# A modulation vector by products on VectorE instead of column sums on TensorE, and eleven matmuls of ones at the start

## The chip, the cores and the metric

The kernel runs on one core of a Trainium2 chip. The metric is the device time of one execution in microseconds (us), shown as the median of several runs.

## The reference, cut to what matters

Three blocks run one after the other on a sequence of 512 tokens with 1024 features: two layers of the first block (grouped-query band attention, short convolution, gated mix, SwiGLU feed-forward) and one layer of the second block, whose two halves are modulated by a vector that depends on an input `c` alone.

```
c_act = jax.nn.silu(c)
mod = c_act @ ada_w[l] + ada_b[l]          # c: 1024, ada_w: 1024 x 6144
sh_a, sc_a, gt_a, sh_m, sc_m, gt_m = jnp.split(mod, 6)
h = rmsnorm(x, norm_mix_g) * (1.0 + sc_a) + sh_a
...
x = x + gt_a * mixed
```

The change concerns `mod`, 6144 values, and nothing else of what is computed.

## The kernel before, in words

Activations lie with features on the partitions (tiles of 128 features x 512 tokens). Each weight matrix comes as units of 128x1024 fp32 words (512 KB). `Stream` loads a unit into one of three raw buffers (L255, queue of SyncE, SP), ScalarE makes its high part `wh` (L267), VectorE the remainder `wl` (L268), two units ahead of their use. A block of 128 output features (`mblock`, `mm_kb`) is 24 matmuls of 128x512: for each of eight tiles of the input the three products high x high (L523), low x high (L524) and high x low (L525).

The program is written in one order, and a scheduler then places each engine's instructions by a simulated timeline. So instructions stand on the engines in another order than in the source, and a small change of the source can move rows elsewhere. PSUM tiles outside attention take their buffers from two groups in the cycle of `CYC` (L331), one step for each tile that `ps` hands out.

`setup` (L338) issues the first loads: some columns, the first weight unit, four tiles of the input `x`, two more units, constants. It fills a 128x128 tile `ones` (L357). `ada_start` (L895) makes `ca`, silu of `c` as 8 columns of 128, by seven short VectorE operations and one Exp on ScalarE (`sigmoid_small`, L383).

The modulation is spread over `ffn1` (L706), the feed-forward part of each layer of the first block. It loops over 22 tiles of the hidden width, each with two blocks: the gate (L718 on VectorE times the norm, SiLU on ScalarE, L720 on GpSimd), and the up projection (L723 product, L516 the low part). In tiles 2 to 13 of each layer `ada_step` (L906) is called twice, 48 times in all. One step takes a tile `adaraw` of 128x1024 (128 rows of `ada_w`, 1024 of its columns), multiplies each partition by its value of `ca` and adds the result to `adaacc` (L918 for the first of eight, L920 for the other seven), then loads the next tile (L934). After eight steps the sum over the 128 partitions is still open: eight matmuls with `adaacc` as the stationary operand and one column of `ones` as the moving one (L927) give 8 columns of 128 sums, and VectorE adds the bias (L930). Six such groups, three in each layer, give `mod` as 128 x 48. The profile counts each fp32 matmul as two instructions.

Tiles of 128x1024 words, `adaraw` and `adaacc` among them, come from one pool of 39 buffers (`blk`).

Of the kernel before, what the change touches and what calls it, by code (L numbers as in the profile page):

```python
# [9 lines left out]
F32 = mybir.dt.float32  # L10
F32R = mybir.dt.float32r
AF = mybir.ActivationFunctionType
OP = mybir.AluOpType

P = 128
T = 512
D = 1024
NB = 8
# [5 lines left out]
NF = FF // P  # L24
# [4 lines left out]
U = 1024  # L29
# [3 lines left out]
def col_layout():  # L33
    off, lay = 0, {}

    def add(name, n):
        nonlocal off
        lay[name] = (off, n)
        off += n

    for l in range(DEPTH):
        for n in ("g_pre_mix", "g_post_mix", "g_pre_ffn", "g_post_ffn"):
            add(f"{n}{l}", NB)
        add(f"conv_w{l}", 3 * NB)
        add(f"sink{l}", NH)
    for n, c in (("c", NB), ("ada_b", 48), ("nmg", NB), ("nfg", NB), ("fcw", 3 * NF), ("fcb", NF), ("dgq", 1),
                 ("dgk", 1), ("lam", P), ("subg", 1), ("fgq", 1), ("fgk", 1), ("fbf", 4), ("ngq", 1), ("ngk", 3),
                 ("pe", 32)):
        add(n, c)
    return lay, off  # L50
# [9 lines left out]
def fm_cols(v):  # L60
    v = np.asarray(v)
    return v.reshape(-1, P).T
# [20 lines left out]
def pack(inp):  # L83
# [20 lines left out]
    o = np.cumsum([0, 256, 256, 256, 256, 256, 256, 4, 256, 256, 256, 256, 64, 64, 64, 64, 64, 64, 12])  # L104
# [7 lines left out]
    g = cat(dvs, dvw, bf, dg, dks, dkw)  # L112
    g = np.concatenate([g.reshape(NB, P, 272), np.zeros((1, P, 272), g.dtype)]).reshape(3, 3, P, 272)
    g = g.transpose(0, 2, 1, 3).reshape(3, P, 816)
# [7 lines left out]
    put(np.stack([fm_units(up[:, :FF]), fm_units(up[:, FF:])], axis=1).reshape(2 * NF, P, U))  # L122
    put(down_units(inp["ffn_w_down_2"][0]))
    lay, nc_ = col_layout()
    cols = np.zeros((P, nc_), np.float32)

    def setc(name, v):
        o, n = lay[name]
        cols[:, o:o + n] = v

    for l in range(DEPTH):
# [1 line left out]
            setc(f"{n}{l}", fm_cols(inp[n][l]))  # L133
        setc(f"conv_w{l}", fm_cols(inp["conv_w"][l]))
        setc(f"sink{l}", np.tile(inp["attn_sink"][l][None, :], (P, 1)))
    setc("c", fm_cols(inp["c_2"][0]))
    setc("ada_b", fm_cols(inp["ada_b_2"][0]))
    setc("nmg", fm_cols(inp["norm_mix_g_2"][0]))
    setc("nfg", fm_cols(inp["norm_ffn_g_2"][0]))
# [36 lines left out]
    for i in range(2):  # L176
# [4 lines left out]
    c, s = np.cos(ang).astype(np.float32).T, np.sin(ang).astype(np.float32).T  # L181
# [12 lines left out]
        "onehot": onehot,  # L194
        "tab": np.ascontiguousarray(tab, np.float32),
        "phi": phib.reshape(P, 32 * P),
        "ada": np.asarray(inp["ada_w_2"])[0].reshape(NB, P, 6, U).transpose(2, 0, 1, 3).reshape(48, P, U),
        "x": np.ascontiguousarray(np.asarray(inp["x"])[0].T.reshape(NB, P, T).transpose(1, 0, 2).reshape(P, NB * T)),
    }

# [79 lines left out]
class Kern:  # L280
# [31 lines left out]
    def small(self, name, shape, dt=F32, bufs=3):  # L312
        return self.smp.tile(shape, dt, name=self.n(name), tag=name, bufs=bufs)

    TAIL = 4
    NHF = 4
    NH3 = 4
# [20 lines left out]
    def setup(self):  # L338
        nc = self.nc
        self.cols = self.cpool.tile([P, self.ncol], F32, name="cols")  # L340
        nc.sync.dma_start(self.cols[:, :NB], self.a["cols"][:, :NB])
        xin = self.a["x"].rearrange("p (j a t) -> p j a t", j=4, a=2)
        self.xsrc = [[xin[:, j, :, t0:t1] for j in range(4)] for t0, t1 in HV]
        self.xpre = {}
        self.st.load_to(1)
        for j in range(4):
            self.xpre[0, j] = self.xload(0, j)
        self.st.load_to(3)
        self.cst = self.cpool.tile([P, 520], F32, name="cst")
        nc.sync.dma_start(self.cst, self.a["consts"])  # L350
        nc.sync.dma_start(self.cols[:, NB:], self.a["cols"][:, NB:])
        self.ident = self.cst[:, 0:P]
        self.band = self.cst[:, P:512]
        self.caus = self.cst[:, 384:512]
        self.valid = self.cst[:, 512:520]
        self.ones = self.cpool.tile([P, P], F32, name="ones")
        nc.vector.memset(self.ones, 1.0)  # L357
        self.mhalf = self.cpool.tile([P, 4], F32, name="mhalf")
        nc.vector.memset(self.mhalf, -0.5)
        self.R = self.cpool.tile([P, T], F32, name="R")  # L360
# [179 lines left out]
    def layer(self, l, tail, pend):  # L540
# [130 lines left out]
        acc = self.tmp("acc")  # L671
        m0 = NB - self.TAIL
        for m in range(m0):
# [219 lines left out]
        return F  # L893

    def ada_start(self):  # L895
        nc = self.nc
        self.ca = self.cpool.tile([P, NB], F32, name="ca")
        o, _ = self.lay["c"]
        c = self.cols[:, o:o + NB]
        self.sigmoid_small(self.ca, c, [P, NB])  # L900
        nc.vector.tensor_mul(self.ca, self.ca, c)
        self.mod = self.cpool.tile([P, 48], F32, name="mod")
        self.ada_i = 0
        self.ada_raw = None

    def ada_step(self):  # L906
        nc = self.nc
        i = self.ada_i
        if i >= 48:
            return  # L910
        self.ada_i += 1
        if i == 0:
            self.ada_load(0)
        t = self.ada_raw
        g, kb = divmod(i, NB)
        if kb == 0:
            self.ada_acc = self.blk("adaacc", [P, U], F32)
            nc.vector.tensor_scalar(self.ada_acc, t, self.ca[:, 0:1], None, op0=OP.mult)  # L918
        else:
            nc.vector.scalar_tensor_tensor(self.ada_acc, t, self.ca[:, kb:kb + 1], self.ada_acc, op0=OP.mult,  # L920
                                           op1=OP.add)
        if i + 1 < 48:
            self.ada_load(i + 1)
        if kb == NB - 1:
            ps = self.ps("ada")
            for m in range(NB):
                nc.tensor.matmul(ps[:, m:m + 1], self.ada_acc[:, m * P:(m + 1) * P], self.ones[:, 0:1], start=True,  # L927
                                 stop=True)
            o = self.lay["ada_b"][0] + g * NB
            nc.vector.tensor_add(self.mod[:, g * NB:(g + 1) * NB], ps[:, :NB], self.cols[:, o:o + NB])  # L930

    def ada_load(self, i):
        self.ada_raw = self.blk("adaraw", [P, U], F32)
# [258 lines left out]
    def block2(self, tail, pend):  # L1192
# [185 lines left out]

        m0 = NB - self.TAIL
        for m in range(m0):  # L1380
# [401 lines left out]
```

## Time and profile before

| | before |
|---|---|
| median of 3 runs | 2462.95 us (2461.41 to 2464.72) |
| the profiled execution | 2465.88 us |
| its span, first to last instruction | 2464.2 us |
| mean granted TensorE clock | 0.991 |
| busy: TensorE matmul | 2407.3 us (98%) |
| TensorE weight loads (beside the matmuls) | 2073.7 us (84%) |
| VectorE | 1324.1 us (54%) |
| ScalarE | 996.1 us (40%) |
| GpSimd | 399.2 us (16%) |

PE is the TensorE matmul, PEld its weight load, DVE VectorE, ACT ScalarE, POOL GpSimd and SPq the queue of SyncE that issues the DMAs. A row of the timeline gives start, duration, engine, line, operation, output and inputs, and a count where equal rows are merged; in square brackets stands the idle time before it and what ended it. Matmuls are pipelined: on a busy TensorE the step from one start to the next is the cost, not the duration.

### The profile page before, as it was taken

How to read it: one execution, taken by the hardware profiler on the slowest of the kernel's cores; microseconds unless marked ns; L12 is line 12 of the kernel's file. 1: busy time of each engine (PE TensorE's matmuls, PEld its weight loads, DVE VectorE, ACT ScalarE, POOL GpSimd, SP SyncE). 2: the span in 40 equal slices, each digit the busy share in tenths (PEclk: the TensorE clock that was granted, in tenths of full speed). 3: DMA queues.
4: the chain of work that ended last, by engine and by line, in shares of the span. 5: the costliest groups of instructions: out<-in, count | busy, mean ns of one | idle time of the engine just before them, and what ended most of it. 6: DMA issues, size and time to landing. Idle time of an engine off the chain costs nothing.

```text
span 2464.2 us, 32671 instructions
## 1 busy us (share of the span) xinstructions
PE 2407.3 (98%) x12680; PEld 2073.7 (84%) x12680; DVE 1324.1 (54%) x2324; ACT 996.1 (40%) x1808; POOL 399.2 (16%) x437
## 2 busy tenths in 40 slices
PE   8999999999999999999999999999898899999999
PEld 8888888888888898888888888888788878888888
DVE  6777544366533177775434655422667586644531
ACT  4555423442223245554224322322375575333420
POOL 3433001211110034230012111100021232000000
PEclk9999999999999999999999999999799999999999
DMA  4511523355423244223233553332221204233350
GB/s 159 149 61 64 165 94 103 103 196 200 149 85 121 80 144 126 69 83 99 94 98 129 181 195 137 99 107 74 91 88 53 83 22 146 78 103 103 105 171 24
DMA packets 90115, 272.77 MB, mean 111 GB/s; under 512 B 10175, under 2 KB 19007, under 8 KB 89960
## 3 DMA queue, kind: packets, MB, share of 16 engines
q1 hardware_dynamic: 89960, 270.68, 33.1%
q8 instruction: 100, 1.64, 0.3%
q14 instruction: 55, 0.45, 0.1%
HBM read 249.65 MB, written 15.22 MB: 107 GB/s over the span
## 4 chain that ended last, share of the span: by engine, by line
PE 90%; DVE 3%; ACT 3%; POOL 2%; issue 2%; DMA 0%; SPq 0%; POOLq 0%; ACTq 0%; DVEq 0%
PE ps L523 24%; PE ps L525 24%; PE ps L524 24%; PE hd L524 2%; PE hd L525 2%; PE hd L523 2%; PE o L840 2%; PE pt L815 1%; PE tm L1025 1%; PE tm L1026 1%; PE tm L1027 1%; POOL t L576 1%; POOL t L575 1%; ACT pp L378 1%; PE s L791 1%
## 5 line engine op out<-in xcount | busy, mean ns | idle before, releaser
L268 DVE TENSOR_TENSOR wl<-raw,wh 128x1024 fp32r<-128x1024 f32 x382 | 477.5, 1267 | 346.6 <-ACT wh L267 283.2
L267 ACT CAST wh<-raw 128x1024 fp32r<-128x1024 f32 x382 | 390.0, 1050 | 188.6 <-DMA raw<-in_w_dram 99.0
L525 PE MATMUL ps<-hh,wl 128*128 128x512 f32 x752 | 295.3, 393 | 0.9 <-DVE wl L268 0.8
L524 PE MATMUL ps<-hl,wh 128*128 128x512 f32 x752 | 294.9, 392 | 0.0
L523 PE MATMUL ps<-hh,wh 128*128 128x512 f32 x752 | 294.4, 392 | 0.0
L524 PE MATMUL ps<-hfl,wh 128*128 128x512 f32 x640 | 249.3, 390 | 0.0
L523 PE MATMUL ps<-hfh,wh 128*128 128x512 f32 x640 | 249.1, 390 | 0.0
L525 PE MATMUL ps<-hfh,wl 128*128 128x512 f32 x640 | 248.9, 389 | 0.0
L525 PEld LDWEIGHTS ps<-hh,wl 128*128 128x128 f32 x752 | 141.3, 188 | 29.1 <-DVE wl L268 2.1
L524 PEld LDWEIGHTS ps<-hl,wh 128*128 128x128 f32 x752 | 141.2, 188 | 27.2
L523 PEld LDWEIGHTS ps<-hh,wh 128*128 128x128 f32 x752 | 141.2, 188 | 27.1 <-ACT ot L844 0.2
L525 PE MATMUL ps<-hidh,wl 128*128 128x512 f32 (+1 forms) x396 | 145.1, 366 | 0.0
L523 PE MATMUL ps<-hidh,wh 128*128 128x512 f32 (+1 forms) x396 | 144.9, 366 | 0.0
L524 PE MATMUL ps<-hidl,wh 128*128 128x512 f32 (+1 forms) x396 | 144.7, 365 | 0.0
L378 ACT ACTIVATE pp<-pp,at_nm 128x256 f32<-128x256 f32 (+1 forms) x208 | 114.4, 553 | 68.2 <-DVE at_nm L797 60.0
L525 PEld LDWEIGHTS ps<-hfh,wl 128*128 128x128 f32 x640 | 120.1, 188 | 24.9
L524 PEld LDWEIGHTS ps<-hfl,wh 128*128 128x128 f32 x640 | 120.2, 188 | 24.7
L523 PEld LDWEIGHTS ps<-hfh,wh 128*128 128x128 f32 x640 | 120.0, 188 | 24.8
L720 POOL TENSOR_TENSOR gs<-gs,R 128x512 f32<-128x512 f32 x44 | 71.4, 1623 | 377.6 <-ACT gs L378 366.6
L524 PE MATMUL ps<-h3l,wh 128*128 128x512 f32 x320 | 124.5, 389 | 0.0
L525 PE MATMUL ps<-h3h,wl 128*128 128x512 f32 x320 | 124.5, 389 | 0.0
L523 PE MATMUL ps<-h3h,wh 128*128 128x512 f32 x320 | 124.3, 389 | 0.0
(461 smaller groups left out, 5200.3 us busy)
## 6 DMA issues: line engine op xcount, KB each, us to landing
raw<-in_w_dram SPq DMA_DIRECT2D x382, 512.0 KB, 3.7
adaraw<-in_ada_dram SPq DMA_DIRECT2D x48, 512.0 KB, 5.6
xd<-xh SPq DMA_DIRECT2D x24, 256.0 KB, 2.1
xh<-xd SPq DMA_DIRECT2D x24, 256.0 KB, 3.1
xh<-in_x_dram SPq DMA_DIRECT2D x16, 256.0 KB, 5.0
Q<-ql SPq DMA_DIRECT2D x32, 128.0 KB, 3.4
bias_d<-row_d SPq DMA_DIRECT2D x8, 320.0 KB, 7.5
KH<-kst SPq DMA_DIRECT2D x16, 128.0 KB, 3.9
```

Of the source, the lines that this page charges most:

```text
L267: nc.scalar.copy(hi, raw)
L268: nc.vector.tensor_sub(lo, raw, hi.bitcast(F32))
L378: i = nc.scalar.activation(out, in_, func, **kw)
L523: nc.tensor.matmul(ps[:, t], w[0][:, sl], h.hi[kb][:, t], start=first, stop=False)
L524: nc.tensor.matmul(ps[:, t], w[0][:, sl], h.lo[kb][:, t], start=False, stop=False)
L525: nc.tensor.matmul(ps[:, t], w[1][:, sl], h.hi[kb][:, t], start=False, stop=last)
L575: nc.gpsimd.tensor_mul(t2, t2, S)
L576: nc.gpsimd.tensor_add(t1, t1, t2)
L720: nc.gpsimd.tensor_mul(g, g, self.R)
L791: nc.tensor.matmul(ps[:, :n], q, KL[g][:, LO[i]:HI[i]], start=False, stop=True)
L815: nc.tensor.transpose(bank[:, c0:c0 + P], pslice(h, i)[:, c:c + P], self.ident)
L840: nc.tensor.matmul(ps[:, c0:c1], V[j][:, g * P:(g + 1) * P], t[b][:, a, c0:c1], start=(a == 0 and j == 0), stop=(a == 1 and j == 2))
```

## The change

The matrix `ada_w` is laid out transposed: tile i holds 128 of the 6144 output features on the partitions, and the 1024 inputs along the free axis. `c` comes as one row of 1024 words (`crow`) and is spread over all partitions by the DMA that loads it, once in each layer; SiLU is one operation of ScalarE on 128x1024. One step is then one VectorE instruction, `tensor_tensor_reduce`: product of the two tiles, summed along the free axis starting from the bias column, the sum going straight into a column of `mod`. The seven short operations of `ada_start`, the matmuls of L927 and the adds of L930 are gone. Apart from that, `setup` now issues eleven matmuls of `ones` by `ones` (128x128, fp32) into a PSUM tile `pw` that nobody reads.

```diff
+    WARM = 11
...
         nc.vector.memset(self.ones, 1.0)
+        ps = self.ps("pw")
+        for i in range(self.WARM):
+            nc.tensor.matmul(ps[:, :P], self.ones, self.ones, start=True, stop=True)
...
     def ada_start(self):
-        nc = self.nc
-        self.ca = self.cpool.tile([P, NB], F32, name="ca")
-        o, _ = self.lay["c"]
-        c = self.cols[:, o:o + NB]
-        self.sigmoid_small(self.ca, c, [P, NB])
-        nc.vector.tensor_mul(self.ca, self.ca, c)
         self.mod = self.cpool.tile([P, 48], F32, name="mod")
         self.ada_i = 0
-        self.ada_raw = None
...
         self.ada_i += 1
-        if i == 0:
-            self.ada_load(0)
+        if i % 24 == 0:
+            self.ca = self.blk("ca", [P, U], F32)
+            self.nc.sync.dma_start(self.ca, self.a["crow"].to_broadcast([P, U]))
+            self.act(self.ca, self.ca, AF.Silu)
+            self.ada_load(i)
         t = self.ada_raw
-        g, kb = divmod(i, NB)
-        if kb == 0:
-            self.ada_acc = self.blk("adaacc", [P, U], F32)
-            nc.vector.tensor_scalar(self.ada_acc, t, self.ca[:, 0:1], None, op0=OP.mult)
-        else:
-            nc.vector.scalar_tensor_tensor(self.ada_acc, t, self.ca[:, kb:kb + 1], self.ada_acc, op0=OP.mult,
-                                           op1=OP.add)
-        if i + 1 < 48:
+        if i % 24 < 23:
             self.ada_load(i + 1)
-        if kb == NB - 1:
-            ps = self.ps("ada")
-            for m in range(NB):
-                nc.tensor.matmul(ps[:, m:m + 1], self.ada_acc[:, m * P:(m + 1) * P], self.ones[:, 0:1], start=True,
-                                 stop=True)
-            o = self.lay["ada_b"][0] + g * NB
-            nc.vector.tensor_add(self.mod[:, g * NB:(g + 1) * NB], ps[:, :NB], self.cols[:, o:o + NB])
+        o = self.lay["ada_b"][0] + i
+        self.nc.vector.tensor_tensor_reduce(out=t, in0=t, in1=self.ca, scale=1.0, scalar=self.cols[:, o:o + 1],
+                                            op0=OP.mult, op1=OP.add, accum_out=self.mod[:, i:i + 1])
```

Three places show how the instructions stand now. Behind the added lines of `setup` the line numbers are four higher than before (L527 is L523 of before), behind `ada_start` lower.

TensorE at the start of the program, before (`hd` is the output of the first three blocks, `hh` and `hl` the parts of the normalised input):

```order
L1777 UNCONDITIONAL_BRANCH
L523 MATMUL hd_168<-hh_10_122,wh_8_116 128x256
L524 MATMUL hd_168<-hl_11_123,wh_8_116 128x256
L525 MATMUL hd_168<-hh_10_122,wl_9_117 128x256
L523 MATMUL hd_168<-hh_10_122,wh_8_116 128x256
```

The same place now:

```order
L1765 UNCONDITIONAL_BRANCH
L361 MATMUL pw_99<-ones 128x128 x11
L527 MATMUL hd_168<-hh_9_122,wh_7_116 128x256
L528 MATMUL hd_168<-hl_10_123,wh_7_116 128x256
L529 MATMUL hd_168<-hh_9_122,wl_8_117 128x256
```

The eleven matmuls stand ahead of all others on TensorE; behind them the order is as it was.

TensorE in `ffn1` of the first layer around the first of the six groups, before (`ps` is the PSUM tile of a block, `hfh` and `hfl` its input):

```order
L524 MATMUL ps_5131<-hfl_762_4474,wh_842_5039 128x512
L525 MATMUL ps_5131<-hfh_761_4473,wl_843_5040 128x512
L523 MATMUL ps_5131<-hfh_761_4473,wh_842_5039 128x512
L927 MATMUL ada_5115<-ones,adaacc_4878 128x1 x8
L524 MATMUL ps_5131<-hfl_762_4474,wh_842_5039 128x512
L525 MATMUL ps_5131<-hfh_761_4473,wl_843_5040 128x512
```

The same place now:

```order
L528 MATMUL ps_5124<-hfl_761_4475,wh_841_5042 128x512
L529 MATMUL ps_5124<-hfh_760_4474,wl_842_5043 128x512
L527 MATMUL ps_5159<-hfh_746_4431,wh_845_5077 128x512
L528 MATMUL ps_5159<-hfl_747_4432,wh_845_5077 128x512
L529 MATMUL ps_5159<-hfh_746_4431,wl_846_5078 128x512
```

Nothing stands between the matmuls of the blocks any more.

VectorE at the first steps of the modulation, before (each `wl` is a weight unit that a block of TensorE waits for):

```order
L718 TENSOR_TENSOR gs_4916<-ps_4891,R 128x512
L918 TENSOR_SCALAR adaacc_4878<-adaraw_4876,ca 128x1024
L268 TENSOR_TENSOR wl_821_4886<-raw_4687,wh_820_4885 128x1024
L920 SCALAR_TENSOR_TENSOR adaacc_4878<-adaraw_4880,ca,adaacc_4878 128x1024
L268 TENSOR_TENSOR wl_825_4921<-raw_4693,wh_824_4920 128x1024
L920 SCALAR_TENSOR_TENSOR adaacc_4878<-adaraw_4883,ca,adaacc_4878 128x1024
L723 TENSOR_TENSOR hidf_4951<-ps_4926,gs_4916 128x512
L268 TENSOR_TENSOR wl_831_4962<-raw_4843,wh_830_4961 128x1024
```

The same place now (`ISA` is the product with its sum, the row `mod 128x1` behind it the read of the sum):

```order
L722 TENSOR_TENSOR gs_4919<-ps_4894,R 128x512
L268 TENSOR_TENSOR wl_820_4889<-raw_4688,wh_819_4888 128x1024
L268 TENSOR_TENSOR wl_824_4924<-raw_4694,wh_823_4923 128x1024
L917 ISA adaraw_4880,mod<-adaraw_4880,ca_4877,cols 128x1024
L917 ISA mod 128x1
L917 ISA adaraw_4882,mod<-adaraw_4882,ca_4877,cols 128x1024
L917 ISA mod 128x1
L268 TENSOR_TENSOR wl_830_4965<-raw_4844,wh_829_4964 128x1024
L917 ISA adaraw_4885,mod<-adaraw_4885,ca_4877,cols 128x1024
L917 ISA mod 128x1
L727 TENSOR_TENSOR hidf_4954<-ps_4929,gs_4919 128x512
```

The first two weight units stand ahead of the first step now, the later ones behind two or three steps.

## Rows read from the trace of the kernel before

**Rows 1.** Stretches of ffn1: us, PE, PEld, DVE, ACT, POOL busy (instructions), clock, DMA.

```profile
558.00:620.00 62.00, 62.00 (x291) 51.86 (x290) 39.04 (x41) 15.76 (x21) 9.22 (x6) 1.00 0.55 204
...
682.00:744.00 62.00, 62.00 (x275) 51.35 (x274) 25.00 (x28) 20.51 (x25) 9.27 (x6) 1.00 0.28 93
```

**Rows 2.** What TensorE waited for, whole span: us in total, times, longest.

```profile
PE hd L523 <- ACT hh L447: 6.9, 1, 6.9
...
PE ps L525 <- DVE wl L268: 0.8, 2, 0.5
```

**Rows 3.** Timeline of TensorE around one group of the modulation.

```profile
569.48 0.39 PE L523 MATMUL ps<-hfh,wh 128*128 128x512 f32 x1
...
569.71 1.84 PE L927 MATMUL ada<-ones,adaacc 128*128 128x1 f32 x16
...
571.41 0.49 PE L524 MATMUL ps<-hfl,wh 128*128 128x512 f32 x1
...
571.74 0.40 PE L525 MATMUL ps<-hfh,wl 128*128 128x512 f32 x1
```

**Rows 4.** Instructions on the tile adaacc: ns min/median/max, first and last start, forms.

```profile
L927 PE MATMUL ada<-ones,adaacc x96: 164/250/250, 569.7 to 1519.6; 128*128 128x1 f32 x96
L920 DVE SCALAR_TENSOR_TENSOR adaacc<-adaraw,ca,adaacc x42: 1268/1277/2327, 541.5 to 1512.2; 128x1024 f32<-128x1024 f32 x42
```

**Rows 5.** VectorE by shape, whole span: count, busy us, mean ns, idle before it.

```profile
L268 DVE TENSOR_TENSOR wl<-raw,wh 128x1024 fp32r<-128x1024 f32 x382 | 477.5, 1267 | 346.6 <-ACT wh L267 283.2 <-PE ps L524 35.3 <-issue 22.2
...
L516 DVE TENSOR_TENSOR hidl<-hidf,hidh 128x512 fp32r<-128x512 f32 x44 | 30.4, 690 | 23.7 <-ACT hidh L515 23.3
...
L1145 DVE CUSTOM_DVE_ANT_0 pp<-s,F 128x512 f32<-128x512 f32 x16 | 10.8, 677 | 0.0
...
L1145 DVE CUSTOM_DVE_ANT_0 pp<-s,F 128x256 f32<-128x256 f32 x16 | 6.6, 415 | 0.0
...
L1145 DVE DVE_READ_ACCUMULATOR2_ANT at_m<- 128x1 f32 x80 | 6.3, 79 | 0.0
```

**Rows 6.** Timelines of VectorE and TensorE: the tightest weight unit and its first use.

```profile
540.12 1.49 DVE L268 TENSOR_TENSOR wl<-raw,wh 128x1024 fp32r<-128x1024 f32 x1 [1.04 <-ACT wh L267]
...
543.87 0.39 PE L525 MATMUL ps<-hfh,wl 128*128 128x512 f32 x1
```

**Rows 7.** Timeline of SyncE's queue at the first steps of the modulation.

```profile
530.82 2.06 SPq L934 DMA_DIRECT2D adaraw<-in_ada_dram  x4
541.63 0.33 SPq L255 DMA_DIRECT2D raw<-in_w_dram  x1
```

**Rows 8.** Timeline of the first 30 us: TensorE, and two rows of VectorE.

```profile
0.90 0.17 DVE L357 MEMSET ones<- 128x128 f32 x1 [0.90 <-PEq L1773]
...
11.21 1.87 PE L416 MATMUL pc<-ones,acc 128*128 128x1 f32 x8
12.94 0.56 PE L524 MATMUL hd<-hl,wh 128*128 128x256 f32 x1
...
13.17 1.22 DVE L268 TENSOR_TENSOR wl<-raw,wh 128x1024 fp32r<-128x1024 f32 x1
...
18.63 0.41 PE L523 MATMUL hd<-hh,wh 128*128 128x256 f32 x1
18.85 0.32 PE L524 MATMUL hd<-hl,wh 128*128 128x256 f32 x1
...
19.12 0.28 PE L523 MATMUL hd<-hh,wh 128*128 128x256 f32 x1
19.24 0.28 PE L524 MATMUL hd<-hl,wh 128*128 128x256 f32 x1
...
28.30 0.95 PE L416 MATMUL pc<-ones,acc 128*128 128x1 f32 x8
```

**Rows 9.** A later place where the granted clock fell, columns as in rows 1.

```profile
1345.00:1350.00 5.00, 3.98 (x32) 3.60 (x30) 4.86 (x8) 2.51 (x7) 0.36 (x1) 1.00 0.35 135
1350.00:1355.00 5.00, 4.36 (x26) 4.36 (x27) 5.00 (x13) 4.68 (x10) 0.88 (x1) 0.66 0.73 252
```

More of the change, by code (lines that the diff above doesn't have):

```diff
@@ L45, in col_layout @@
         add(f"sink{l}", NH)
-    for n, c in (("c", NB), ("ada_b", 48), ("nmg", NB), ("nfg", NB), ("fcw", 3 * NF), ("fcb", NF), ("dgq", 1),
+    for n, c in (("ada_b", 48), ("nmg", NB), ("nfg", NB), ("fcw", 3 * NF), ("fcb", NF), ("dgq", 1),
                  ("dgk", 1), ("lam", P), ("subg", 1), ("fgq", 1), ("fgk", 1), ("fbf", 4), ("ngq", 1), ("ngk", 3),
@@ L135, in pack @@
         setc(f"sink{l}", np.tile(inp["attn_sink"][l][None, :], (P, 1)))
-    setc("c", fm_cols(inp["c_2"][0]))
     setc("ada_b", fm_cols(inp["ada_b_2"][0]))
@@ L196, in pack @@
         "phi": phib.reshape(P, 32 * P),
-        "ada": np.asarray(inp["ada_w_2"])[0].reshape(NB, P, 6, U).transpose(2, 0, 1, 3).reshape(48, P, U),
+        "ada": np.ascontiguousarray(np.asarray(inp["ada_w_2"])[0].T.reshape(48, P, U)),
+        "crow": np.ascontiguousarray(np.asarray(inp["c_2"])[0].reshape(1, U)),
         "x": np.ascontiguousarray(np.asarray(inp["x"])[0].T.reshape(NB, P, T).transpose(1, 0, 2).reshape(P, NB * T)),
@@ L895, in ada_start @@
     def ada_start(self):
-        nc = self.nc
-        self.ca = self.cpool.tile([P, NB], F32, name="ca")
-        o, _ = self.lay["c"]
-        c = self.cols[:, o:o + NB]
-        self.sigmoid_small(self.ca, c, [P, NB])
-        nc.vector.tensor_mul(self.ca, self.ca, c)
         self.mod = self.cpool.tile([P, 48], F32, name="mod")
         self.ada_i = 0
-        self.ada_raw = None
     def ada_step(self):
-        nc = self.nc
         i = self.ada_i
```

## The prediction, made before the changed kernel had run

> **What bounds the kernel now.** I read the busy shares first: TensorE's matmuls fill 98% of the span, VectorE 54%. So a gain must come out of TensorE's own queue or out of the 2% in which it stands still. Then I read stretches of 62 us in the stage that changes. In ffn1 TensorE is busy for 62.00 of 62.00 us, VectorE for 39 and ScalarE for 16 [rows 1]. A stretch without modulation holds 275 matmuls of 128x512, so one step is 62/275 = 0.2255 us. The view of what TensorE waited for agrees: for a weight unit's low part it waited 0.8 us in the whole span, and its longest wait of all is the 6.9 us for the first loads [rows 2]. Third came the timeline around one group of the modulation, since in ffn1 each instruction of TensorE adds its step to the span. Last I read the first 30 us, where the eleven matmuls go.
>
> **Matmuls of the modulation, removed.** From L523 before the first group to the second matmul behind it 2.26 us pass (569.48 to 571.74), where two steps would take 0.45. The group costs 1.81 us [rows 3]. The profile counts 96 instructions, six groups of 16 [rows 4], so 6 x 1.81 = 10.9 us leave a full queue. No wait stands there to take their place. The six adds of L930 go with them.
>
> **The product with its sum on VectorE.** The trace has no such instruction with both operands in SBUF. The nearest rows are L1145 with one operand in PSUM: 415 ns for 256 columns, 677 for 512, thus 1.02 ns a column and 153 ns fixed, and 79 ns for the read of the sum [rows 5]. For 1024 columns that makes 1.20 + 0.08 = 1.28 us. The step it replaces, also with two fp32 operands in SBUF, takes 1.277 us [rows 4]. I take 1.28; the lower end is 1.20, the read overlapping, the upper end twice the cost per column, 2.33. Is it covered? A tile of the loop is 48 matmuls, 10.8 us. VectorE has two weight units (2.53), three products of 128x512 (2.07) and two steps in it: 4.6 + 2.56 = 7.2 us, as before. So it costs nothing, and 3.6 us a tile are left. The cover would be gone if a step took over (10.8 - 4.6)/2 = 3.1 us.
>
> One rule of the Trainium skill speaks against the step (Vector Engine (DVE) Microarchitecture Reference, section 7, Points that are easy to get wrong): an instruction of the scalar-tensor-tensor shape with two SBUF sources that are not bf16 runs at half throughput. L920 is of this kind and its 1.277 us show no halving [rows 4], but it sums nothing along the axis, so the rows do not rule it out for the new step. By the rule the step takes the upper end above, and the sum stays while 3.1 us are not reached.
>
> **Order on VectorE and on the queue.** The weight unit with least room was done at 541.61 and used at 543.87 [rows 6]: 2.26 us. It now stands ahead of every step. The units behind it stand behind two and three more steps. At 1.28 us each that is some 3 us more, but a TensorE block takes 24 x 0.2255 = 5.4 us, and each further unit is due a block later. Cost 0; what it would be without that cover is the third rival. On SyncE's queue `ca` and a fifth tile now stand ahead of the next weight unit. Four such issues took 2.06 us, and the next weight issue started 8.7 us later [rows 7]: room for two issues of 0.5 us. The two transfers of `ca` (512 KB each) and two SiLUs fall on a DMA share of 0.55 and a quarter-busy ScalarE [rows 1]: 0.
>
> **The short operations at the start, removed.** Seven VectorE operations on eight columns and an Exp. At no more than the 0.17 us of the memset [rows 8] they make 1.2 us, only two of them ahead of the unit at 13.17. I take 0, with 0.3 us of gain as the other end.
>
> **The matmuls of ones.** The first 18.8 us run at the lower clock, whatever the clock column prints there: matmuls of 128x256 follow every 0.22 us at 18.63 and every 0.12 at 19.12, and eight one-column ones take 1.87 us at 11.21 and 0.95 at 28.30 [rows 8]. That is 1.2 and 2.4 GHz, and the higher level came behind 5.9 us of unbroken work from 12.94. The eleven are 22 instructions. At the 0.234 us of L416 they take 5.1 us, and from the end of the memset (1.07) they end at 6.2, ahead of the first weight unit's matmul at 6.9 [rows 2]. If load and product did not overlap (0.234 + 0.22 each) they would end at 11.1, and some 1.5 us would be lost. What can they give? Of the 27 matmuls from 12.94 to 18.85 each would save 0.1 us: 2.5 us, plus 0.9 for L416: 3.4 at most, somewhat less for the weight unit that is ready only at 14.4. The lower end is 0: between 6.9 and 12.9 TensorE works with gaps, and rows 9 show the clock falling after 1.0 us of idle in a stretch of five. I take 1.0 us, nearer the low end, for that row.
>
> **Rows moved elsewhere.** The added PSUM tile shifts the cycle of buffers, and the scheduler moves rows at the seams between stages, where TensorE does wait. One fall of the clock there costs 5 x (1 - 0.66) = 1.7 us [rows 9]. I allow two more or two fewer, 3.4 us either way, and take 0.
>
> **The sum.** -10.9 - 1.0 = -11.9 us. The profiled execution took 2465.88 us (1.7 around its span), so 2454.0 for one like it. The median of the runs lies 2.9 below it, hence 2462.95 - 11.9 = **2451.0 us**. With the ends, this case reaches from 2462.95 - 10.9 - 3.4 - 3.4 = 2445 to 2462.95 - 10.9 + 1.5 + 3.4 = 2457.
>
> **Rivals.**
> - *The clock stays up from the start.* All 3.4 us come: 2462.95 - 14.3 = 2448.7. For it: the ones end less than 1 us before the first loads' matmuls. Against it: the gaps behind. The Trainium skill (TensorE: Matmul & The Clock Gate, Part 1) calls the low clock the default and says that activity releases it and idling restores it; the step from 0.22 to 0.12 us agrees, and whether gaps as here count as idling no row shows.
> - *The seams give half back.* The shifted rows cost a longer stretch at half clock where the second block starts, 4 to 8 us: 2455 to 2459. For it: that start is where TensorE idles most. Against it: the order there differs by a few dozen rows of matmuls only.
> - *Half rate on VectorE.* A step takes 2.33 us, a tile 9.3 of 10.8. The fifth step of the first burst makes the unit behind it some 5 us later than I count; TensorE waits 0 to 3 us: 2451 to 2454.
> - *VectorE becomes the bound, slower than before.* At 3.6 us a step a tile takes 11.8 us, and 24 tiles lose 24: 2475. It decides from 3.1 us, and passes the old time from 3.1 + 12/48 = 3.35 us. For it: no row with two SBUF operands and a sum. Against it: it needs nearly three times what the nearest rows cost.
>
> **Chances.** Forecast 0.64, clock up 0.15, seams 0.10, half rate 0.08, VectorE the bound 0.03. The range of 8 in 10 is 2445 to 2457.5: forecast, clock and half rate lie in it, with the nearer part of the seams. About 0.2%, 4.9 us, can be told from no change. Faster by more: all but half of the seams and the last, 0.92; within it 0.05; slower 0.03.
>
> **What would show it.** No matmuls stand in ffn1 but those of the blocks, and its stretches hold 275 in 62 us throughout. The product takes 1.2 us and its read 0.08; VectorE's busy time stays near 1324 us. TensorE's wait for `wl` stays under 2 us. Matmuls of 128x256 follow every 0.12 us before 18.8 us. The prediction is wrong if a step takes over 3.1 us, if ffn1 shows idle on TensorE, or if the waits at the start of the second block grow by over 4 us.

## The result, and the profile after

| | before | changed |
|---|---|---|
| median | 2463.84 us (4 runs, 2461.41 to 2466.24) | 2451.38 us (4 runs, 2450.45 to 2452.08) |
| changed / before | | 0.9949, 95% interval 0.9932 to 0.9966 |
| span of the profiled execution | 2464.2 us | 2449.2 us |

The change takes 12.5 us off the median. The forecast was 2451.0 us, in a range of 2445.0 to 2457.5. Code lines of the start are four higher than before, those of the second block twelve lower: L527 to L529 are the matmuls of L523 to L525, L420 is L416, L435 and L431 are L431 and L427, L451 and L452 are L447 and L448.

The page's busy times of the changed kernel:

```profile
PE 2397.2 (98%) x12606; PEld 2064.2 (84%) x12606; DVE 1326.2 (54%) x2359; ACT 996.5 (41%) x1809; POOL 387.2 (16%) x437
```

TensorE has 10 us less to do, with 4.4 us for the ones in it, and VectorE 2 us more. The stretches of ffn1, columns as in [rows 1]:

```profile
558.00:620.00 62.00, 62.00 (x276) 51.34 (x275) 40.88 (x53) 15.81 (x21) 8.44 (x6) 1.00 0.55 204
682.00:744.00 62.00, 62.00 (x276) 51.34 (x275) 26.87 (x30) 20.63 (x25) 7.98 (x5) 1.00 0.34 111
```

The first of these held 291 matmuls, 16 of them the short ones of a group. Now both hold 276: TensorE is as full as before, and every matmul is one of a block. The new instruction, in the view of one line (ns min/median/max, first and last start):

```profile
L917 DVE CUSTOM_DVE_ANT_0 adaraw<-adaraw,ca,cols x48: 1267/1274/2317, 541.2 to 1499.7; 128x1024 f32<-128x1024 f32 x48
L917 DVE DVE_READ_ACCUMULATOR2_ANT mod<- x48: 71/77/85, 542.4 to 1500.9; 128x1 f32 x48
```

And as it stands in VectorE's timeline:

```profile
541.20 1.27 DVE L917 CUSTOM_DVE_ANT_0 adaraw<-adaraw,ca,cols 128x1024 f32<-128x1024 f32 x1
542.41 0.08 DVE L917 DVE_READ_ACCUMULATOR2_ANT mod<- 128x1 f32 x1
542.41 1.27 DVE L917 CUSTOM_DVE_ANT_0 adaraw<-adaraw,ca,cols 128x1024 f32<-128x1024 f32 x1
543.61 0.07 DVE L917 DVE_READ_ACCUMULATOR2_ANT mod<- 128x1 f32 x1
```

The read of the sum starts together with the next step, so a step costs 1.21 us from start to start. The longest duration in the view of L917, 2.317 us, occurs twice among the 48. Both times GpSimd's product of `gs` (L724) was running when the step began; here the row of GpSimd, then the one of VectorE:

```profile
647.98 1.46 POOL L724 TENSOR_TENSOR gs<-gs,R 128x512 f32<-128x512 f32 x1 [10.03 <-ACT gs L382]
648.21 2.32 DVE L917 CUSTOM_DVE_ANT_0 adaraw<-adaraw,ca,cols 128x1024 f32<-128x1024 f32 x1
```

Eight other steps began ahead of such a product and ran beside it; they took their 1.27 us. In the kernel before eight of the 42 steps of L920 took 2.31 to 2.33 us, each begun while that product ran. What TensorE waited for, columns as in [rows 2]:

```profile
PE pb L435 <- DVE dg L431: 5.6, 2, 3.9
...
PE hd L528 <- DVE hl L452: 1.2, 2, 0.9
PE pw L361 <- DVE ones L358: 1.1, 1, 1.1
PE hd L527 <- ACT hh L451: 1.0, 1, 1.0
...
PE ps L529 <- DVE wl L268: 0.3, 1, 0.3
```

For low parts of weights it waits 0.3 us in the whole span. The 6.9 us for the first loads are split in two, with the ones between. TensorE at the start:

```profile
1.12 4.39 PE L361 MATMUL pw<-ones 128*128 128x128 f32 x22 [1.12 <-DVE ones L358]
6.47 0.38 PE L527 MATMUL hd<-hh,wh 128*128 128x256 f32 x1 [0.96 <-ACT hh L451]
7.72 0.39 PE L528 MATMUL hd<-hl,wh 128*128 128x256 f32 x1 [0.86 <-DVE hl L452]
7.94 0.30 PE L529 MATMUL hd<-hh,wl 128*128 128x256 f32 x1
8.06 0.40 PE L527 MATMUL hd<-hh,wh 128*128 128x256 f32 x1
8.26 0.44 PE L528 MATMUL hd<-hl,wh 128*128 128x256 f32 x1
...
10.91 1.87 PE L420 MATMUL pc<-ones,acc 128*128 128x1 f32 x8
...
18.33 0.28 PE L527 MATMUL hd<-hh,wh 128*128 128x256 f32 x1
18.45 0.29 PE L528 MATMUL hd<-hl,wh 128*128 128x256 f32 x1
```

The ones did bring the higher clock: within their row the step falls from 0.213 to 0.112 us at 4.68, behind 3.6 us of unbroken work. TensorE then stands idle for 0.96 and 0.86 us. Behind both, from 7.94 to 8.06, a matmul of 128x256 still takes 0.12 us; from 8.26 on the step is back at 0.21, and L420 takes the 1.87 us of [rows 8]. The higher level returns at 18.3, where it came at 18.9 before.

**A ledger by stage.** TensorE's blocks are the same in all kernels here, so the k-th matmul of a source line in one trace can be set against the k-th in another. The shift of its start, read at seven places, gives what each stretch gained (negative) or lost. Between 541.15 and 671.81 us of before, three groups lie; the same two matmuls start at 540.65 and 665.77 now: 130.66 against 125.12, thus 5.54 us for three groups, 1.85 each. The second layer gives 5.54 again. In the first layer the shift jumps at the place of each group and nowhere else in this stretch by as much as 0.3 us. The whole, against the profile of before (671.81 to 860 and 1550 to 1700 add nothing here; in the table of all profiles below they count with the groups):

| stretch of before (us) | changed |
|---|---|
| 0 to 400, the start | -0.48 |
| 400 to 541, head of the first ffn1 | -0.02 |
| the six groups | -11.08 |
| 860 to 1340, second layer up to its ffn1 | -0.47 |
| 1340 to 1413, head of the second ffn1 | -1.17 |
| 1700 to the end, second block | -1.75 |
| sum | -14.96 |

The two profiled executions differ by 15.0 us, the medians by 12.5. So the groups are 11.1 of 12.5, and the other rows need care, as the experiments show.

### The profile page after: what moved, and what is told of

Its sections match the earlier page's. It is cut to its first block, busy times and chain, and to the rows that moved or that the text cites. A ratio compares the mean times of both kernels' runs of the same rounds, so it can differ in the third digit from the quotient of the medians.

```text
span 2449.2 us, 32493 instructions
## 1 busy us (share of the span) xinstructions
PE 2397.2 (98%) x12606; PEld 2064.2 (84%) x12606; DVE 1326.2 (54%) x2359; ACT 996.5 (41%) x1809; POOL 387.2 (16%) x437
## 4 chain that ended last, share of the span: by engine, by line
PE 92%; ACT 3%; DVE 3%; issue 1%; POOL 1%; DMA 0%; SPq 0%; ACTq 0%; POOLq 0%; DVEq 0%
PE ps L527 24%; PE ps L529 24%; PE ps L528 24%; PE hd L528 2%; PE hd L529 2%; PE hd L527 2%; PE o L844 2%; PE tm L1013 1%; PE pt L819 1%; PE tm L1014 1%; PE tm L1015 1%; ACT pp L382 1%; PE s L795 1%; PE s L794 1%; POOL t L580 0%
## 5 line engine op out<-in xcount | busy, mean ns | idle before, releaser
L268 DVE TENSOR_TENSOR wl<-raw,wh 128x1024 fp32r<-128x1024 f32 x382 | 484.5, 1285 | 348.4 <-ACT wh L267 280.1
L529 PE MATMUL ps<-hh,wl 128*128 128x512 f32 x752 | 295.3, 393 | 0.3 <-DVE wl L268 0.3
L527 PE MATMUL ps<-hh,wh 128*128 128x512 f32 x752 | 294.4, 392 | 0.0
L529 PE MATMUL ps<-hfh,wl 128*128 128x512 f32 x640 | 248.7, 389 | 0.0
L527 PE MATMUL ps<-hfh,wh 128*128 128x512 f32 x640 | 248.4, 389 | 0.0
L529 PEld LDWEIGHTS ps<-hh,wl 128*128 128x128 f32 x752 | 141.3, 188 | 28.2 <-DVE wl L268 1.2
L527 PEld LDWEIGHTS ps<-hh,wh 128*128 128x128 f32 x752 | 141.3, 188 | 27.3 <-ACT ot L848 0.2
L529 PE MATMUL ps<-hidh,wl 128*128 128x512 f32 (+1 forms) x396 | 145.1, 366 | 0.0
L527 PE MATMUL ps<-hidh,wh 128*128 128x512 f32 (+1 forms) x396 | 144.9, 366 | 0.0
L382 ACT ACTIVATE pp<-pp,at_nm 128x256 f32<-128x256 f32 (+1 forms) x208 | 114.4, 553 | 67.9 <-DVE at_nm L801 59.9
L527 PEld LDWEIGHTS ps<-hfh,wh 128*128 128x128 f32 x640 | 120.0, 188 | 25.0
L529 PEld LDWEIGHTS ps<-hfh,wl 128*128 128x128 f32 x640 | 120.1, 188 | 24.7
L529 PE MATMUL ps<-h3h,wl 128*128 128x512 f32 x320 | 124.5, 389 | 0.0
L527 PE MATMUL ps<-h3h,wh 128*128 128x512 f32 x320 | 124.2, 389 | 0.0
L724 POOL TENSOR_TENSOR gs<-gs,R 128x512 f32<-128x512 f32 x44 | 63.5, 1442 | 375.6 <-ACT gs L382 364.7
```

The lines of the kernel that those rows point to most:

```text
L268: nc.vector.tensor_sub(lo, raw, hi.bitcast(F32))
L382: i = nc.scalar.activation(out, in_, func, **kw)
L527: nc.tensor.matmul(ps[:, t], w[0][:, sl], h.hi[kb][:, t], start=first, stop=False)
L529: nc.tensor.matmul(ps[:, t], w[1][:, sl], h.hi[kb][:, t], start=False, stop=last)
L724: nc.gpsimd.tensor_mul(g, g, self.R)
```

## The experiments

**One half of the change at a time.** Three kernels: the modulation without the ones, the ones without the modulation, and the kernel before with the cycle of PSUM buffers moved by one step and nothing else.

```diff
 # mod_alone: the changed kernel without
-        ps = self.ps("pw")
-        for i in range(self.WARM):
-            nc.tensor.matmul(ps[:, :P], self.ones, self.ones, start=True, stop=True)
 # ones_alone: the kernel before with
+        ps = self.ps("pw")
+        for i in range(11):
+            nc.tensor.matmul(ps[:, :P], self.ones, self.ones, start=True, stop=True)
 # cycle_alone: the kernel before with
+        ps = self.ps("pw")
```

> The new modulation without the matmuls of ones and without their PSUM tile. Theory A (the gain is the six groups, 1.85 us each in the ledger of the two traces, and the ones give next to nothing): -11.1 us from the groups, 0 to -0.3 at the start, and whatever the seams do, up to 3.4 us either way: 0.9940 to 0.9968 of before, the middle at 2452.5. In its trace each group is worth 1.85 us again, and the first matmul of 128x256 at a step of 0.12 us comes at about 18.6 us. Theory B (the ones give 1 us or more, as forecast or as the rival of the raised clock has it): the start is 1 to 3.4 us longer than in the changed kernel, 2453.4 to 2456.

> The kernel before with the eleven matmuls of ones and their PSUM tile, its modulation unchanged. Theory A: the start gains 0.2 to 0.5 us; the whole differs from before by that and by the seams, 2460 to 2467. Theory B: -1 to -3.4 us from the start alone. In either case the trace tells them apart at the first block's end, before any seam: shift 0.2 to 0.5 against 1 or more.

> The kernel before with the PSUM tile handed out and nothing written to it: only the cycle of the buffers moves by one step. Theory A (rows moved at the seams make the 3.4 us that the ledger does not give to groups or start): no shift in the first 300 us, no shift within ffn1, steps of up to 2 us at the seams (stage ends near 490, 880, 1350 and 1720 us and in the second block), the sum anywhere from -3.4 to +3.4. Theory B (a moved cycle costs and gives nothing; the seams gain because of the modulation itself): the shift stays within 0.3 us everywhere.

| kernel | median us (runs) | to before, 95% interval |
|---|---|---|
| before, in this comparison | 2464.05 (21) | |
| modulation alone | 2451.35 (5) | 0.9947, 0.9935 to 0.9959 |
| ones alone | 2462.68 (11) | 0.9990, 0.9981 to 0.9999 |
| PSUM cycle alone | 2462.59 (11) | 0.9993, 0.9984 to 1.0002 |

Without the ones the changed kernel takes the same time (2451.35 and 2451.38), and with the ones the kernel before takes the time of the one with the cycle alone (2462.68 and 2462.59). **Eleven matmuls of ones, with the rows that they move, give nothing that can be measured.** The modulation, with the rows that it moves, gives all of it. Several hundred rows of TensorE stand in another order in each pair, so a small gain of the ones that moved rows take back is not ruled out. The PSUM cycle alone shows shifts of up to 1.5 us at the seams in its profile, and 1.0 us in all, as its theory A has it; but the same kernel shifts as much from one execution to the next (below), so the cycle is not shown to be the cause. The profile of the modulation alone is not quite as expected, though. Without any ones the start gained not 0 to 0.3 but 3.07 us (the ledger of all profiles stands further down):

```profile
6.55 0.58 PE L523 MATMUL hd<-hh,wh 128*128 128x256 f32 x1 [6.55 <-ACT hh L447]
7.79 0.58 PE L524 MATMUL hd<-hl,wh 128*128 128x256 f32 x1 [0.67 <-DVE hl L448]
...
10.98 1.16 PE L416 MATMUL pc<-ones,acc 128*128 128x1 f32 x8
12.00 0.36 PE L524 MATMUL hd<-hl,wh 128*128 128x256 f32 x1
12.20 0.28 PE L525 MATMUL hd<-hh,wl 128*128 128x256 f32 x1
12.32 0.28 PE L523 MATMUL hd<-hh,wh 128*128 128x256 f32 x1
```

The 0.12 us step is there from 12.2 us on, almost seven us earlier than in [rows 8], with idle like that of before ahead of it. So the start's clock is not a matter of the ones alone.

**The same kernel again.**

> The changed kernel once more, instruction for instruction, with a second profile. Theory A (the places at which the clock falls are not a matter of the kernel alone: the same gap of about 1 us costs a stretch at half clock in one execution and none in the next): the six groups and ffn1 stand as they did to 0.1 us, but the first step of 0.12 us comes at another time than 18.3 us, or a half-clock stretch appears or goes at the gaps near 494 and 1343 us, and the span differs from 2449.2 by 1 to 4 us. Theory B (each kernel has its own fixed places): the same stretches at the same gaps, span within 0.5 us.

Median 2451.79 us (5 runs, 2450.67 to 2454.44). Three stretches of the first profile and the same three of the second, columns as in [rows 1], first the changed kernel:

```profile
8.00:18.00 10.00, 9.85 (x45) 9.27 (x45) 9.74 (x27) 9.59 (x20) 0.69 (x1) 0.50 1.01 353
490.00:500.00 10.00, 8.34 (x66) 7.91 (x65) 10.00 (x22) 8.09 (x17) 0.88 (x1) 1.00 0.50 169
1340.00:1350.00 10.00, 8.34 (x66) 7.91 (x65) 10.00 (x21) 8.51 (x18) 0.88 (x1) 1.00 0.56 187
```

and its second execution:

```profile
8.00:18.00 10.00, 9.77 (x63) 9.04 (x64) 9.89 (x27) 10.00 (x21) 0.70 (x1) 0.83 1.01 367
490.00:500.00 10.00, 8.48 (x55) 8.14 (x55) 10.00 (x20) 8.60 (x17) 0.88 (x1) 0.83 0.65 214
1340.00:1350.00 10.00, 8.34 (x55) 7.92 (x55) 9.91 (x21) 8.10 (x17) 0.88 (x1) 0.83 0.63 200
```

The instructions are the same and the idle of TensorE is the same to 0.14 us, but the granted clock (third from the end) is not: 0.50 against 0.83 at the start, 1.00 against 0.83 at the two heads of ffn1, where TensorE waits 0.99 us in both. Theory A holds, but for one thing: the spans should have differed by 1 to 4 us, and they agree, since one gain and two losses cancel (2449.2 and 2449.0). This is what the ledger shows for all profiles, each against the one profile of before:

| kernel | start | 400 to 541 | groups | 860 to 1340 | 1340 to 1413 | second block | sum |
|---|---|---|---|---|---|---|---|
| changed | -0.48 | -0.02 | -11.08 | -0.47 | -1.17 | -1.75 | -14.96 |
| changed, again | -2.85 | 1.45 | -11.08 | -0.47 | -0.05 | -2.20 | -15.18 |
| modulation alone | -3.07 | 1.48 | -11.08 | 0.68 | -1.01 | -1.49 | -14.50 |
| ones alone | 0.53 | -0.03 | 0 | 0.71 | -1.25 | -3.58 | -3.61 |
| PSUM cycle alone | 0.17 | 1.47 | 0 | -0.34 | -1.17 | -1.20 | -1.04 |
| 22 ones | -0.25 | 1.44 | -11.08 | 0.75 | 1.40 | -3.93 | -11.66 |
| 22 ones, again | -2.99 | -0.04 | -11.08 | 0.77 | -1.21 | -5.06 | -19.61 |
| 22 ones and fillers | -2.92 | -0.03 | -11.08 | 0.76 | 0.21 | -1.06 | -14.11 |
| 22 ones alone | -1.60 | 1.44 | 0 | -0.53 | 0.21 | -5.98 | -6.46 |
| 28 ones | -1.80 | 1.21 | -11.08 | 0.75 | -1.21 | -5.81 | -17.92 |
| step twice | 0.46 | 1.44 | -11.08 | -0.29 | 0.11 | -1.96 | -11.32 |
| step three times | -0.84 | 1.40 | -6.74 | -0.32 | 0.25 | -3.84 | -10.08 |
| cast behind dg | -0.73 | 1.45 | -11.08 | -0.46 | 0.14 | -5.27 | -15.95 |

In three columns the same kernel is found at both ends: the start (0.5 to -3.1), the head of the first ffn1 (about 0, or 1.2 to 1.5) and of the second (-1.2, about 0, 1.4). At 860 to 1340 the value goes with the kernel: about 0.7 where the order of rows leaves 1.2 us of idle at the layer's seam, -0.3 to -0.5 where it doesn't. The second block has a section of its own below. In the groups column six groups are worth 11.08 us in each of the profiles that lost them and whose VectorE was not overloaded.

**VectorE's room.** The product is issued twice or three times a step, the extra ones into a tile that nobody reads.

```diff
+        self.nc.vector.tensor_tensor_reduce(out=self.junk, in0=t, in1=self.ca, scale=1.0, scalar=self.cols[:, o:o + 1],
+                                            op0=OP.mult, op1=OP.add, accum_out=self.mod2[:, i:i + 1])
```

> The changed kernel with each product and sum of the modulation issued twice, the first time into a tile that nobody reads (96 in place of 48); the order on TensorE is the same but for two rows. Theory A (the cover of the prediction: 4.6 us of other work on VectorE in a tile of 10.8 us): a step costs 2.56 us, a tile 9.7 of 10.8, and nothing is lost: within 1 us of the changed kernel, TensorE full in ffn1. Theory B (VectorE's room is less than the sum says, units come late in the bursts of steps): TensorE waits for the low parts at L529, 1 to 5 us over both layers. VectorE's busy time grows by 48 x 1.28 = 61 us in either case.

> The changed kernel with each product and sum issued three times (144), two of them into a tile that nobody reads. Theory A (the point from which VectorE is the bound is 3.1 us a step, by the prediction's third and fourth rivals): at 3.83 us a tile takes 4.6 + 7.7 = 12.3 us on VectorE against 10.8 on TensorE, 1.5 us are lost in each of 24 tiles, 36 us in all, less a few us for units that are ready ahead: 2475 to 2490, VectorE full through the tiles with steps. Theory B (there is more slack than the sum says, steps run on behind the tiles that issue them): under 15 us lost.

Twice: 2452.86 us (5 runs, 2451.17 to 2454.27), with nothing lost in ffn1. The median is 1.1 us above the 2451.79 of the changed kernel beside it, a little outside theory A; in the ledger the groups are whole, and what differs stands in the columns that change from one execution to the next. Three times: 2455.0 us (4 runs, 2453.76 to 2456.02), and 11.08 - 6.74 = 4.3 us of the groups' gain are lost, not 36. The stretch 558 to 620 with the product twice:

```profile
558.00:620.00 62.00, 62.00 (x275) 51.36 (x274) 59.88 (x83) 18.75 (x24) 9.01 (x6) 1.00 0.57 208
```

and three stretches with the product three times:

```profile
558.00:620.00 62.00, 62.00 (x275) 51.32 (x274) 61.93 (x84) 17.41 (x23) 7.60 (x5) 1.00 0.50 176
620.00:682.00 62.00, 61.97 (x273) 50.67 (x272) 61.89 (x84) 18.14 (x23) 8.80 (x6) 1.00 0.44 151
682.00:744.00 62.00, 60.60 (x268) 49.82 (x267) 40.88 (x51) 21.51 (x27) 9.15 (x6) 1.00 0.34 111
```

Twice is below the 3.1 us a step at which the prediction saw the cover gone: VectorE is busy for 59.9 of 62 us and TensorE never waits. Three times is past it: VectorE is full for 124 us, yet TensorE loses 1.4 us in these stretches and 4.3 us over both layers. What the tiles with steps can't hold runs on into the tiles behind them: the last product starts at 1549.1 us instead of 1499.7. The weight units get through between. So room counts over the whole run of tiles and what lies ready ahead, and not tile by tile.

**How many ones, and where they end.**

```diff
-    WARM = 11
+    WARM = 22        # w22, w22_again; 28 in w28
 # w_fill: 22, and in the first block
+    FILL = {2: (2, 3), 4: (2, 2)}       # tile of features: ones ahead of it, ones behind its first matmul
 # ones22_alone: the kernel before with range(22) in the loop of ones_alone
```

> The changed kernel with 22 matmuls of ones. They end at about 7.8 us, behind the two waits of 0.96 and 0.86 us between which the clock fell back in the changed kernel; the first matmul of the first block goes 1.3 us later. Theory A (clock and loads both bind: ScalarE and VectorE are full in 6 to 12 us): the clock stays up for some us longer, TensorE then waits for parts of the input instead, and the start gains 0 to 1 us on the changed kernel. Theory B (the clock is all): 2.0 to 2.5 us gained. Theory C (the later first matmul is on the path): 0.5 to 1.3 us lost.

> The kernel with 22 matmuls of ones once more, beside the changed kernel on the same chip. Theory A (22 are enough to reach the first work, and give back 1 to 3 us of the low clock): median 1 to 3.5 us under that of the changed kernel in this call. Theory B (its lower median was the scatter of five runs): within 1 us of it.

> 22 matmuls of ones as above, and nine more of them put into the four waits of the first block between 8.5 and 11.4 us (two and three at its third tile of features, two and two at its fifth). The order behind them also moves a little. Theory A (the waits for the loads are what lets the clock fall at 11.6 us): the level of 0.12 us a step holds through 11.6 to 18.4 us, and the start gains up to 2.5 us on the 22 alone, less what TensorE then waits for ScalarE and VectorE, which are full there: 0.5 to 2.5 us. Theory B (the clock is up but the loads bind): the start gains less than 0.5 us. Theory C (the fillers push work back): it loses 0.3 to 1 us.

> The kernel before with 22 matmuls of ones, its modulation unchanged; its order has the cast of pastr ahead of dg, as before. Theory A (22 matmuls help through the start's clock by 1 to 3 us): 2460 to 2462 in the median, and a start shifted by -0.2 to -3.0 us in the profile. Theory B (the 22 were faster through the order at the second block alone, and the start depends on the execution, not on the matmuls): within 1 us of the kernel with the PSUM tile alone, 2461.6 to 2463.6.

> The changed kernel with 28 matmuls of ones; its order has the cast of pastr behind dg, as with 22. Theory A (once the ones reach the first work, more of them only push it back, and the clock holds until the waits behind): within 1.5 us of the kernel with 22, 2446 to 2449. Theory B (the longer unbroken work holds the clock through the waits): the start is -2.5 us or better in the profile and the median 2445 to 2447. Theory C (it delays the first block): 2449 to 2452.

| kernel | median us (runs) | lowest to highest | to before, 95% interval |
|---|---|---|---|
| changed, 11 ones (beside the next three) | 2451.79 (5) | 2450.67 to 2454.44 | 0.9951, 0.9938 to 0.9963 |
| 22 ones | 2448.18 (5) | 2447.23 to 2453.90 | 0.9937, 0.9924 to 0.9949 |
| 22 ones, again | 2446.80 (5) | 2445.32 to 2447.57 | 0.9928, 0.9916 to 0.9941 |
| 22 ones and nine fillers | 2451.73 (5) | 2449.41 to 2454.24 | 0.9948, 0.9935 to 0.9960 |
| 28 ones | 2447.16 (5) | 2446.77 to 2447.64 | 0.9927, 0.9915 to 0.9939 |
| 22 ones on the kernel before | 2460.55 (11) | 2456.17 to 2463.40 | 0.9981, 0.9972 to 0.9989 |

With 22 or 28 ones the kernel is 3 to 5 us faster than the changed one. The second comparison of 22 with 11 gives 5.0 us, more than its theory A allowed, and the 28 come out where their theory A has them. On the kernel before, 22 ones give 2460.55 us, 2.1 less than eleven (2462.68, in another comparison). The start of the better execution with 22:

```profile
1.12 7.82 PE L361 MATMUL pw<-ones 128*128 128x128 f32 x44 [1.12 <-DVE ones L358]
8.69 0.36 PE L527 MATMUL hd<-hh,wh 128*128 128x256 f32 x1
8.89 0.28 PE L528 MATMUL hd<-hl,wh 128*128 128x256 f32 x1
```

The ones join the first work, and here the clock held. In the other execution with 22 it fell at 11.6 us, behind waits of 0.2 to 0.3 us. The fillers, which close these waits, held it too, and the start gained 2.92; yet their median is no better than with eleven. So the start is not the main thing. By the table, starts with 22 or 28 gain 1.66 us in the mean of four profiles, with eleven 0.65 (six), with none 0.97 (three, before itself at 0): too few to tell apart.

Not even the raised clock is sure. In three of the six profiles with eleven ones the step fell to 0.112 us while they ran. In the other three it stayed at 0.21 to their end, as in the kernel with the cast moved (below), which has the same order on TensorE as the changed one:

```profile
1.12 5.07 PE L361 MATMUL pw<-ones 128*128 128x128 f32 x22 [1.12 <-DVE ones L358]
```

There a step of 0.12 us came only at 17.5. What the profiles of the kernels near 2447 us have in common is a large gain in the second block, 3.9 to 5.8 us. And the granted clock of the whole execution, which is on record for every run, is higher: 0.994 in all five with 28 ones, 0.993 or 0.994 in the second five with 22, against 0.989 to 0.992 in the nine of the changed kernel. Within the first five with 22 it goes from 0.990 in the slowest to 0.994 in the fastest.

**The second block.** In the changed kernel with 22 or 28 ones and no fillers, and in that with the eleven ones alone, the order of one VectorE row came out differently. VectorE in the changed kernel, between the column sums of the norm (`rs_v`) and `dg`, which TensorE waits for:

```profile
1714.64 0.16 DVE L424 TENSOR_SCALAR rs_v<-pc 128x2 f32<-128x2 f32 x1 [1.15 <-PE pc L420]
1717.74 0.29 DVE L959 CAST pastr<-consts 128x256 fp32r<-128x256 f32 x1 [2.95 <-DMA consts<-in_consts_dram]
1717.95 0.42 DVE L431 TENSOR_TENSOR dg<-cst,rs_r 128x256 f32<-128x256 f32 x1
```

and with 22 ones:

```profile
1720.94 0.16 DVE L424 TENSOR_SCALAR rs_v<-pc 128x2 f32<-128x2 f32 x1 [1.96 <-PE pc L420]
1721.90 0.43 DVE L431 TENSOR_TENSOR dg<-cst,rs_r 128x256 f32<-128x256 f32 x1 [0.80 <-POOL rs_r L402]
1723.22 0.29 DVE L959 CAST pastr<-consts 128x256 fp32r<-128x256 f32 x1 [0.89 <-DMA consts<-in_consts_dram]
```

The cast of a constant waits for its transfer, and in the changed kernel `dg` stands behind it: 2.95 us against 0.80. The test moves that one row and leaves all other rows of every engine in their order. It puts the cast behind the `dg` of the second half of the tokens, at 1745.35 us; with 22 ones it stands behind the one of the first half:

```diff
-        nc.vector.tensor_tensor(dg[:, :n * P].rearrange("p (a b) -> p a b", a=n),
+        self.dg = nc.vector.tensor_tensor(dg[:, :n * P].rearrange("p (a b) -> p a b", a=n),
...
-        nc.vector.tensor_copy(self.pastr, c2[:, P:384])
+        self.order(nc.vector.tensor_copy(self.pastr, c2[:, P:384]), self.dg)
```

> The changed kernel with one row moved: on VectorE the cast of pastr, which waits for a transfer of constants, stands behind the last dg of the second block's start instead of ahead of it; TensorE's order is the same row for row. Theory A (that cast is what makes TensorE's wait for dg at L435 3.9 us in the changed kernel and 1.6 us in the two kernels whose order has it behind): the wait falls to 1.6 us, 2.3 us are gained and perhaps 1.7 more where the half-clock stretch there is shorter: 2447 to 2450. Theory B (the kernel with 22 matmuls of ones is faster by its start alone): no change, 2451 to 2452.5.

The wait went as theory A says, from 5.6 us with a longest of 3.9 to:

```profile
PE pb L435 <- DVE dg L431: 3.2, 2, 1.6
```

and the second block gained 5.27 us where it gained 1.75 and 2.20 in the two profiles of the changed kernel. The five profiles with the cast behind `dg` gained 3.6 to 5.8 there, six with the cast ahead 1.1 to 2.2. But 22 ones alone and the step three times have the cast ahead, with a longest wait of 3.0 us, and gained 6.0 and 3.8 all the same. So the row is not all of it. The granted clock of the stretch 1700 to 1800 goes with the gain too: 0.86 for gains of 1.1 and 1.2, 0.88 for 1.8 and 2.0, 0.90 for 1.5 to 6.0, and 0.91 for 5.1 to 5.8. The changed kernel and then that with the cast moved (us, PE busy, clock, DMA):

```profile
1700.00:1800.00 100.00, 86.33 (x635) 0.88 0.32 106
1700.00:1800.00 100.00, 88.33 (x659) 0.91 0.34 113
```

The median with the cast moved, though, is 2450.59 us (5 runs, 2449.17 to 2453.05), 0.8 to 1.2 below the changed kernel, between the two theories, and the granted clock of its five executions is 0.990 to 0.993, not that of the kernels near 2447 us. **Left open:** that the row's place makes the wait is shown, its worth in the median is not. How the 3 to 5 us of the 22 ones divide between that row, the start and other rows that moved (several hundred on TensorE) is not settled either.

## Why the prediction was right

The mechanism of the main term was right, and so was the room for the product; that the time was met to 0.4 us is luck.

- **The groups, -10.9: right.** The ledger gives 6 x 1.85 = 11.1 us, and full stretches of 276 matmuls.
- **The product on VectorE, 1.28 us: right, at its lower end.** It takes 1.274 us, 1.21 from start to start. The rule cited from the Trainium skill (Vector Engine (DVE) Microarchitecture Reference, section 7, Points that are easy to get wrong) would have made it 2.33 by the prediction's estimate; the median of 48 shows no halving with two fp32 operands in SBUF. Two steps did take 2.32, each begun while a product of GpSimd ran, and 46 with the same operands did not. The rival of the half rate falls with it.
- **Cover: right, and larger than the prediction said.** 2.4 us a step cost nothing. The condition of the last rival, over 3.1 us a step, did not occur in the changed kernel, and the test shows that its price was too high: it counted a loss in every tile from 3.1 us on, 24 us at 3.6, and three products a step (at least 3 x 1.21 = 3.6) lost 4.3 of the 24 us. It added tiles where it should have added the whole run of them.
- **Order on VectorE and SyncE, 0: right.** TensorE's wait for `wl` is 0.3 us.
- **The short operations, 0 with 0.3 at the other end: not told apart.** The first matmul of the first block starts at 6.55 us without them and without ones, at 6.86 before; but with them and the PSUM cycle alone it starts at 6.46.
- **The ones, -1.0: wrong.** The step that failed is that a start closer to full clock would survive the gaps in part. The ones ended at 5.5 us, earlier than the 6.2 estimated, since their last part already ran at the higher clock (with the cast moved they ended at 6.2). Behind 0.96 and 0.86 us of idle the level was lost again, and the medians show 0 for the ones and the rows that they move (0.03 and 0.09 us in two comparisons). The 3.4 us at most were the right size: where the clock came up early, the start gained 2.9 to 3.1.
- **The rival of the raised clock** nearly occurred at the start, in the second execution of the same kernel (2.85 of its 3.4 us, with the lower level from 8.0 to 11.5 us) and without any ones in another kernel (3.07). The prediction took it for a property of the kernel; it is one of the execution. The Trainium skill (TensorE: Matmul & The Clock Gate, Part 1) says that the moment of the rise varies between runs, since the chip's own timing does not begin with the kernel. In the two executions of the changed kernel the first rise came at 4.7 us, and the second, behind the fall, at 18.3 and 11.5. So the trace agrees that it varies; the reason no run here shows.
- **The seams, 0 within 3.4: right as a bound.** 12.46 - 11.08 = 1.4 us of the medians are neither groups nor ones. The kernel with the PSUM cycle alone came out 1.5 us under before with no other change, its interval reaching to 1.0002. So a reordering of that size may be the rest; the runs don't show it. The rival in which the seams give half back did not occur: in no profile did the second block lose.

The change was forecast at -11.9 us and measured at -12.5: the ones' 1.0 us did not come, 1.4 us of rest that had been set at 0 did, and the groups gave 0.2 more. The median of before, from which the forecast subtracts, was 2462.95 us then and is 2463.84 with the fourth run. These offset each other down to 0.4 us.

## What to carry to other kernels

A matmul with one moving column is not cheap on TensorE: 16 such instructions took 1.85 us of a full queue, each about half of what a step of 512 columns takes (0.2255 us), while VectorE could do the same sum within its idle time. Double the moved work to see how much room there is. Matmuls ahead of the first work gave nothing here where idle followed them; where they reached the first work the kernel was faster, by a cause that is not settled. Judge them by medians, against the same kernel without them and with its order of rows looked at. Before a stage's gain is read from two profiles, profile one of the kernels twice and set the same instructions against each other stage by stage: what moves there is not the change's.

## What the hardware showed that was not expected

- One kernel, two executions: with the same idle of 0.99 us, the granted clock stayed at its higher level in one (1.00 in the stretch 490 to 500) and fell to the lower one for 3.4 us in the other (0.83). Over the profiles here such a fall costs 1.0 to 1.5 us at a head of ffn1, and starts of the same kernel differ by up to 2.7 us, more than most terms of this sum. What decides it is left open here.
- A product with its sum along the free axis costs VectorE little more than a plain operation of the same shape: 1.20 to 1.21 us from start to start for 1024 columns, against 1.14 (median) for the subtraction of the weight units where the next operation follows at once. What the product costs without the sum was not measured.
- A step of the modulation that begins while GpSimd's product of `gs` runs takes 2.3 us in place of 1.27, in the changed kernel (2 of 2) and before (8 of 8); one that begins first keeps its time (8 of 8 in the changed kernel).
- VectorE at 61.9 of 62 us, twice in a row, cost TensorE 0.03 us in those stretches, and most of the 2.3 us lost in that layer came behind them: an engine can be full for a while and not be the bound.
